# The channel factors of the first norm inside the split of x

## The chip, the core and the metric

The kernel runs on one core of a Trainium2 chip. The metric is the device time of one execution in microseconds, as the median of several. The core has five engines with a queue of instructions each: TensorE (PE; the loading of its stationary operand is shown apart as PEld), VectorE (DVE), ScalarE (ACT), GpSimd (POOL) and SyncE (SP), which here only issues DMA transfers. An engine takes its instructions in order, and waits where an operand isn't ready.

## The reference, cut to what matters

One transformer block on x of 1024 positions by 1024 channels, in float32. The change lies in the first norm and in the first projections:

```python
def rms_norm(x, g):
    y = x * lax.rsqrt(jnp.mean(x * x, axis=-1, keepdims=True) + EPS)
    return y * g

z = rms_norm(h, attn_norm) @ w_in                 # 1024 x 1024 @ 1024 x 2856
o_nsa = nsa_mixer(...)                            # compressed, selected and window attention, 8 heads
o_gla = gla_mixer(...)                            # gated linear attention, 4 heads
h = h + concat([o_nsa, o_gla]) @ w_out
u = causal_dwconv(rms_norm(h, ffn_norm) @ w_up, conv_w, conv_b)
gate, up = split(u)
h = h + (silu(gate) * up) @ w_down
```

## The kernel before

x is read transposed: a row tile `t` (8 of them, 128 positions each) lies in the core's memory as 128 partitions by 8 groups `k` of channels by 128 positions, so that the channel of a value is given by partition and group. `again` holds the factors of the norm in the same layout, 128 x 8. A product in nearly float32 is made of three products of the type float32r: each operand is split into a high part (`hi_of`, a copy on ScalarE that rounds to float32r, L57) and a low part (`lo_of`, value minus high part, L60, on VectorE or POOL), and `zmm` (L114 to L120) sums high times high (L118), high times low (L119) and low times high (L120) over the eight groups.

The norm's factor per row isn't applied to x: `x_stat` forms the sum of squares of a tile (a reduction on VectorE, L264; a product with ones, L265) and the root by a chain of small instructions on VectorE (`rsqrt`, L66 to L73), and `rx[:, t]` scales the results when they leave PSUM (`kcvc` L289, `gl` L290, `zqk` L201, `vv` L204). The factor per channel is applied to x before the split.

`x_first(t, eng)` (L248 to L259) makes the split tile `xt`: one transfer of 512 KB by SP into `xraw` (2 buffers), the squares `xsq` on ScalarE (1 buffer), the multiply of `xraw` by `again` in place on `eng` (VectorE for tile 0, POOL for the other seven), and then two halves of four groups each, split into high and low part by ScalarE and VectorE.

The stage around it first loads the weights `wA` (296 columns) in four pieces of two groups each, splits them (the low parts on VectorE and POOL in turn), and loads tile 0 ahead of the split of the first piece. Then it loads the eight pieces of `wC` (512 columns; low parts in turn on POOL and VectorE). In the loop over tiles it makes tile `t + 2` and its sum of squares, multiplies tile `t` by `wA` and by `wC`, evicts the results, and stores the split tile to `x_d` for later passes. The later passes (queries, linear attention, attention, and the feed-forward part) read `x_d` and don't call `x_first`.

The order in which an engine takes its instructions isn't that of the text: a scheduler lays out the queues from its own timing of the whole program, so instructions of later steps can stand ahead of earlier ones. Buffers are bound the same way; a load into a buffer waits for the last reader of what was there.

Of the kernel before, what the change touches and what calls it, by code (L numbers as in the profile page):

```python
# [7 lines left out]
F = mybir.dt.float32  # L8
R = mybir.dt.float32r
I32 = mybir.dt.int32  # L10
AF = mybir.ActivationFunctionType
OP = mybir.AluOpType
# [5 lines left out]
NT, NK = 8, 8  # L18
# [16 lines left out]
def body(tc, I, out, tap=lambda name, ap: None):  # L35
    nc = tc.nc
    V, A, P, T, SY = nc.vector, nc.scalar, nc.gpsimd, nc.tensor, nc.sync
# [18 lines left out]
    def hi_of(dst, src, scale=1.0):  # L56
        A.activation(dst, src, AF.Copy, scale=scale)  # L57

    def lo_of(dst, src, hi, eng=None):
        (eng or V).tensor_sub(dst, src, hi.bitcast(F))  # L60
# [19 lines left out]
    again = con.tile([128, NK], F, name="again")  # L80
# [8 lines left out]
    def split(dst_h, dst_l, src, eng=None):  # L89
        hi_of(dst_h, src)  # L90
        lo_of(dst_l, src, dst_h, eng)
# [5 lines left out]
    xtp = pool(sW, "xtp", XB)  # L97
# [60 lines left out]
    with ExitStack() as sp:  # L158
# [70 lines left out]
        def pair(t, z, qpass, kept=[]):  # L229
            kept.append((t, z))  # L230
            if len(kept) == 2:
                for (tt, zz), rr in zip(kept, norms([z for _, z in kept], 8 if qpass else 4)):
                    heads(tt, zz, rr, qpass)
                kept.clear()


        with ExitStack() as sx:
            wap = pool(sx, "wap", 1)
            xr_p = pool(sx, "xr_p", 2)
            xfp = pool(sx, "xfp", 2)  # L240
            ones = wap.tile([128, 1], F, name="ones")
            V.memset(ones, 1.0)
            wah = wap.tile([128, NK, NA], R, name="wah")
            wal = wap.tile([128, NK, NA], R, name="wal")
            WA = [(wah[:, k], wal[:, k]) for k in range(NK)]
            xts = {}

            def x_first(t, eng):  # L248
                raw = xr_p.tile([128, NK, 128], F, name="xraw")
                SY.dma_start(raw, I["xT"][t])  # L250
                sq = xr_p.tile([128, NK, 128], F, name="xsq", bufs=1)
                A.activation(sq, raw, AF.Square)
                eng.tensor_tensor(raw, raw, again[:, :, None].to_broadcast([128, NK, 128]), op=OP.mult)
                xt = []
                for i in range(2):
                    x = (xfp if i else xtp).tile([128, 2, 4, 128], R, name="xt")
                    split(x[:, 0], x[:, 1], raw[:, 4 * i:4 * i + 4], V)
                    xt.append(x)
                return xt, sq  # L259

            def x_stat(t, sq):
                st = pp.tile([128, 512], F, name="st", tag="h1", bufs=2)
                ssq = c2.tile([128, 128], F, name="ssq", tag="vv")
                V.tensor_reduce(ssq, sq.rearrange("p k t -> p t k"), axis=X, op=OP.add)  # L264
                T.matmul(st[:, 0:1], ssq, ones, start=True, stop=True)  # L265
                rsqrt(c2, rx[:, t:t + 1], st[:, 0:1], 1.0 / D, 1)

            for k2 in range(4):
                raw = wap.tile([128, 2, NA], F, name="araw", bufs=2)
                SY.dma_start(raw, I["wA"][k2])  # L270
                ks = slice(2 * k2, 2 * k2 + 2)
                if k2 == 0:
                    SY.dma_start(again, I["again"])
                    xts[0], sq = x_first(0, V)
                split(wah[:, ks], wal[:, ks], raw, P if k2 % 2 else V)
            x_stat(0, sq)
            WC = [w_load(I["wC"][1, k], 512, V if k % 2 else P) for k in range(NK)]
            for dst, name in ((ident, "ident"), (rope, "rope"), (hgain, "hgain")):
                SY.dma_start(dst, I[name])
            xts[1], sq = x_first(1, P)  # L280
            x_stat(1, sq)
            for t in range(NT):
                if t + 2 < NT:
                    xts[t + 2], sq = x_first(t + 2, P)
                    x_stat(t + 2, sq)
                xt = xts.pop(t)
                ps = zp.tile([128, 512], F, name="z")
                zmm(ps[:, :NA], xt, WA)
                V.tensor_scalar(kcvc[:, t], ps[:, :256], rx[:, t:t + 1], None, op0=OP.mult)  # L289
                V.tensor_scalar(gl[:, t], ps[:, 256:NA], rx[:, t:t + 1], None, op0=OP.mult)  # L290
                zq = zp.tile([128, 512], F, name="z")
                zmm(zq, xt, WC)
                for i in range(2):
                    A.dma_start(x_d[t, i].bitcast(F), xt[i].bitcast(F))
                pair(t, evac(t, zq, False), False)
            V.tensor_scalar(rxh, rx, 0.5, None, op0=OP.mult)
            V.tensor_scalar(rx8, rx, 0.125, None, op0=OP.mult)
# [89 lines left out]
        for t in range(NT):  # L387
            xt = x_load(x_d[t])
# [271 lines left out]
    k2 = pool(sK, "k2", 18, side="right")  # L660
# [30 lines left out]
    with ExitStack() as sp:  # L691
# [5 lines left out]
        for half in (1, 0):  # L697
            WO = WO_[half]
            for t in range(NT):
                if half and t in (4, 7):  # L700
                    WO_[0].append([w_load(I["wO"][t // 7, k], 512, V) for k in range(4)])
                if half and t == 7:

                    w0 = [facp["T3"].tile([128, 4, 512], R, name=f"w0{p}", tag=p) for p in "hl"]
                    for i in range(4):
                        raw = rawp.tile([128, 512], F, name="wraw")
# [3 lines left out]
                xt = xtp.tile([128, 2, 4, 128], R, name="xt")  # L710
# [432 lines left out]
```

## Time and profile before

| | |
|---|---|
| median of 3 executions | 1365.21 us (1365.13 to 1858.76) |
| the profiled execution | 1363.89 us |
| its span, first to last instruction | 1362.1 us |
| TensorE, VectorE busy | 96%, 79% of the span |
| ScalarE, POOL busy | 51%, 25% of the span |
| mean granted clock of TensorE | 0.991 of full speed |

The profile is of one execution. An engine's busy time is the union of its instructions; matmuls are pipelined, so a matmul's duration is longer than the distance to the next one, and the same holds by a little for VectorE and ScalarE. An idle stretch is put down to what ended it (the "releaser").

### The profile page before, as it was taken

The numbers are of one execution on the slowest core, as the hardware profiler recorded it, in microseconds if no ns is written. First come the engines' busy times: TensorE is split into PE (matmuls) and PEld (weight loads), VectorE is DVE, ScalarE is ACT, GpSimd is POOL, SyncE is SP. The second block draws the span as 40 slices with busy tenths as digits, with TensorE's granted clock in tenths as the row PEclk, the third lists the DMA queues.
The fourth block names the chain that finished last, engine by engine and source line by source line (L and its number), as shares of the span: only waits on it lengthen the run. The fifth ranks groups of instructions, "written<-read, shape, count | busy, mean of one in ns | idle before, by whom it ended". The sixth has DMA issues, their size and how long they took to land.

```text
span 1362.1 us, 19780 instructions
## 1 busy us (share of the span) xinstructions
PE 1312.4 (96%) x6618; PEld 1096.7 (81%) x6618; DVE 1077.5 (79%) x2530; ACT 701.0 (51%) x1383; POOL 334.0 (25%) x491
## 2 busy tenths in 40 slices
PE   6899989999999999999999999999999998999998
PEld 5787867888788887778788888888888886888887
DVE  7985865877878788982588998888788878699774
ACT  5342655767666567763464544444344444444431
POOL 4343653556644447432500000000000000000000
PEclk9999989999999999999999999999999998999999
DMA  8537673323422225012743122222222229664073
GB/s 306 199 109 263 180 243 101 106 91 117 138 66 83 73 81 157 31 46 67 246 145 112 50 105 93 77 78 94 85 86 76 79 78 349 243 203 155 34 238 115
DMA packets 80535, 177.07 MB, mean 130 GB/s; under 512 B 10785, under 2 KB 22962, under 8 KB 80434
## 3 DMA queue, kind: packets, MB, share of 16 engines
q1 hardware_dynamic: 54450, 111.84, 24.1%
q0 software_dynamic: 10368, 37.75, 9.0%
q10 hardware_dynamic: 15616, 26.22, 5.3%
q8 instruction: 52, 0.85, 0.3%
q14 instruction: 49, 0.40, 0.1%
HBM read 133.84 MB, written 41.94 MB: 129 GB/s over the span
## 4 chain that ended last, share of the span: by engine, by line
PE 82%; DVE 10%; DMA 3%; ACT 3%; issue 2%; POOL 1%; SPq 0%; ACTq 0%; POOLq 0%; DVEq 0%
PE pda L982 9%; PE pdb L982 7%; PE z L118 4%; PE z L119 4%; PE z L120 4%; PE O L466 4%; PE S L448 4%; PE pt L459 3%; PE uZ L679 3%; PE uX L680 3%; PE uX L679 3%; PE uX L681 3%; PE uZ L680 3%; PE uZ L681 3%; PE uW L680 3%; PE uW L681 3%
## 5 line engine op out<-in xcount | busy, mean ns | idle before, releaser
L118 PE MATMUL z<-whi,xt 128*128 128x512 f32 (+1 forms) x384 | 142.8, 372 | 6.5 <-DVE rs_i L67 2.8
L119 PE MATMUL z<-wlo,xt 128*128 128x512 f32 (+1 forms) x384 | 140.4, 366 | 0.1
L120 PE MATMUL z<-whi,xt 128*128 128x512 f32 (+1 forms) x384 | 140.1, 365 | 0.0
L60 DVE TENSOR_TENSOR PTl<-pt,PTh 128x512 fp32r<-128x512 f32 (+1 forms) x148 | 99.9, 684 | 32.8 <-ACT PTh L57 32.4
L453 ACT ACTIVATE P<-P,m 128x640 f32<-128x640 f32 (+7 forms) x128 | 94.1, 735 | 53.5 <-DVE m L450 52.1
L57 ACT ACTIVATE PTh<-pt 128x512 fp32r<-128x512 f32 (+1 forms) x148 | 85.3, 592 | 53.1 <-PE pt L459 50.4
L527 POOL TENSOR_SCALAR P<-P,sc 128x640 f32<-128x640 f32 (+7 forms) x128 | 89.4, 709 | 84.3 <-DVE sc L473 55.5
L448 PE MATMUL S<-kst,qst 128*128 128x320 f32 (+5 forms) x384 | 100.1, 352 | 3.9 <-DVE m L450 3.5
L57 ACT ACTIVATE wuh<-wuraw 128x512 fp32r<-128x512 f32 x65 | 40.5, 631 | 103.3 <-PE uZ L680 52.8
L118 PEld LDWEIGHTS z<-whi,xt 128*128 128x128 f32 x384 | 74.2, 193 | 17.3 <-issue 5.1
L459 PE MATMUL pt<-ident,P 128*128 128x128 f32 x528 | 86.5, 274 | 0.8 <-DVE PTl L60 0.6
L119 PEld LDWEIGHTS z<-wlo,xt 128*128 128x128 f32 x384 | 73.9, 193 | 9.9 <-DVE wlo L60 0.5
L120 PEld LDWEIGHTS z<-whi,xt 128*128 128x128 f32 x384 | 73.9, 192 | 9.9
L57 ACT ACTIVATE dh<-g 128x1024 fp32r<-128x1024 f32 x44 | 46.6, 1062 | 65.6 <-PE pdb L982 27.7
L57 ACT ACTIVATE wuh<-ws 128x512 fp32r<-128x512 f32 x76 | 47.6, 631 | 63.2 <-PE uW L680 29.2
L459 PEld LDWEIGHTS pt<-ident,P 128*128 128x128 f32 x528 | 66.1, 141 | 15.9 <-issue 1.4
L448 PEld LDWEIGHTS S<-kst,qst 128*128 128x128 f32 x384 | 62.5, 191 | 13.7 <-DVE m L450 8.1
L982 PE MATMUL pda<-dh 128*128 128x512 f32 x176 | 68.5, 390 | 0.0
L982 PE MATMUL pda<-dh,dl 128*128 128x512 f32 x176 | 68.4, 390 | 0.0
L982 PE MATMUL pda<-dl,dh 128*128 128x512 f32 x176 | 68.4, 390 | 0.0
L792 ACT ACTIVATE y<-u,cb,cw 128x1024 f32<-128x1024 f32 x44 | 54.3, 1240 | 20.9 <-DVE u L871 15.1
L450 DVE CUSTOM_DVE_ANT_0 P<-S,wmask 128x320 f32<-128x320 f32 (+4 forms) x96 | 46.0, 485 | 23.9 <-PE S L448 22.7
(474 smaller groups left out, 3956.3 us busy)
## 6 DMA issues: line engine op xcount, KB each, us to landing
xt<-x_d POOLq DMA_DIRECT2D x48, 512.0 KB, 3.7
wuraw<-in_wU_dram SPq DMA_DIRECT2D x42, 512.0 KB, 3.6
dv<-in_wD_dram SPq DMA_DIRECT2D x55, 256.0 KB, 3.2
act_d<-y SPq DMA_DIRECT2D x22, 512.0 KB, 2.6
dv<-act_d SPq DMA_DIRECT2D x44, 256.0 KB, 3.4
x_d<-xt ACTq DMA_DIRECT2D x16, 512.0 KB, 4.1
xt<-mix_d POOLq DMA_DIRECT2D x16, 512.0 KB, 4.1
g<-in_wD_dram SPq DMA_DIRECT2D x22, 256.0 KB, 5.6
```

The source lines that it names most:

```text
L57: A.activation(dst, src, AF.Copy, scale=scale)
L60: (eng or V).tensor_sub(dst, src, hi.bitcast(F))
L118: T.matmul(ps, x[:, 0], wh, start=(k == 0), stop=False)
L119: T.matmul(ps, x[:, 0], wl, start=False, stop=False)
L120: T.matmul(ps, x[:, 1], wh, start=False, stop=(k == NK - 1))
L448: T.matmul(ps[:, :e - c], qst[:, h], kcols(i, c, e), start=(i == 0), stop=(i == 1))
L453: A.activation(Pt, Pt, AF.Exp, bias=m, scale=-1.0, accum_out=sc)
L459: T.transpose(tp[:n, h], get(h), ident)
L527: P.tensor_scalar(Ps[hh][:, :n], Ps[hh][:, :n], sc[:, hh:hh + 1], 1.0, op0=OP.mult, op1=OP.mult)
L680: T.matmul(ps, wh[:, k], bl[:, k], start=False, stop=False, skip_group_check=True)
L681: T.matmul(ps, wl[:, k], bh[:, k], start=False, stop=(k == 3 and last), skip_group_check=True)
L982: T.matmul(ps[t], l[:, ts], r, start=(j == 0 and n == 0 and not add), stop=(j == NH - 1 and n == 2), skip_group_check=True)
```

## The change

`x_first` no longer takes an engine and no longer multiplies the tile. For each of the eight groups of a tile, ScalarE's copy for the high part takes the group's column of `again` as its scale per partition, and VectorE's subtraction becomes a fused instruction, `raw * again - high`. The squares come after the splits in the text. Tile 0 is loaded by two transfers of four groups each, and `again` is loaded ahead of the first piece of `wA`.

```diff
-            def x_first(t, eng):
+            def x_first(t):
                 raw = xr_p.tile([128, NK, 128], F, name="xraw")
-                SY.dma_start(raw, I["xT"][t])
+                xt = []
+                for i in range(2):
+                    ks = slice(4 * i, 4 * i + 4)
+                    if t == 0:
+                        SY.dma_start(raw[:, ks], I["xT"][t, :, ks])
+                    elif i == 0:
+                        SY.dma_start(raw, I["xT"][t])
+                    x = (xfp if i else xtp).tile([128, 2, 4, 128], R, name="xt")
+                    for k in range(4):
+                        g, r = again[:, 4 * i + k:4 * i + k + 1], raw[:, 4 * i + k]
+                        hi_of(x[:, 0, k], r, g)
+                        V.scalar_tensor_tensor(x[:, 1, k], r, g, x[:, 0, k].bitcast(F), op0=OP.mult, op1=OP.subtract)
+                    xt.append(x)
                 sq = xr_p.tile([128, NK, 128], F, name="xsq", bufs=1)
                 A.activation(sq, raw, AF.Square)
-                eng.tensor_tensor(raw, raw, again[:, :, None].to_broadcast([128, NK, 128]), op=OP.mult)
-                xt = []
-                for i in range(2):
-                    x = (xfp if i else xtp).tile([128, 2, 4, 128], R, name="xt")
-                    split(x[:, 0], x[:, 1], raw[:, 4 * i:4 * i + 4], V)
-                    xt.append(x)
                 return xt, sq
...
             for k2 in range(4):
+                if k2 == 0:
+                    SY.dma_start(again, I["again"])
                 raw = wap.tile([128, 2, NA], F, name="araw", bufs=2)
                 SY.dma_start(raw, I["wA"][k2])
                 ks = slice(2 * k2, 2 * k2 + 2)
                 if k2 == 0:
-                    SY.dma_start(again, I["again"])
-                    xts[0], sq = x_first(0, V)
+                    xts[0], sq = x_first(0)
                 split(wah[:, ks], wal[:, ks], raw, P if k2 % 2 else V)
...
-            xts[1], sq = x_first(1, P)
+            xts[1], sq = x_first(1)
             x_stat(1, sq)
             for t in range(NT):
                 if t + 2 < NT:
-                    xts[t + 2], sq = x_first(t + 2, P)
+                    xts[t + 2], sq = x_first(t + 2)
                     x_stat(t + 2, sq)
```

## Rows read from the trace of the kernel before

**Rows 1.** The page: the span, and TensorE's busy time, share and instructions.

```profile
span 1362.1 us, 19780 instructions
PE 1312.4 (96%) x6618; PEld 1096.7 (81%) x6618; DVE 1077.5 (79%) x2530; ACT 701.0 (51%) x1383; POOL 334.0 (25%) x491
```

**Rows 2.** Stretches: bounds and length, busy time by engine, granted clock, DMA share, GB/s.

```profile
0.00:10.00 10.00, 0.00 (x0) 0.00 (x0) 3.60 (x4) 5.41 (x8) 1.80 (x6) 1.00 0.77 251
...
22.00:80.00 58.00, 51.26 (x287) 44.29 (x287) 56.79 (x163) 25.31 (x46) 25.68 (x26) 1.00 0.58 206
80.00:105.00 25.00, 25.00 (x141) 21.83 (x140) 20.71 (x67) 11.22 (x23) 12.26 (x17) 1.00 0.40 136
```

**Rows 3.** Waits of TensorE to 130 us: waiter, releaser, total, times, longest.

```profile
PE z L118 <- ACT xt L57: 10.1, 1, 10.1
...
PE z L118 <- DVE rs_i L67: 2.8, 2, 2.0
PE z L118 <- DVE vv L204: 2.6, 1, 2.6
...
PE z L120 <- DVE xt L60: 1.1, 1, 1.1
```

**Rows 4.** Timeline of the first tile: start, duration, engine, line, out and in.

```profile
1.65 0.42 SPq L250 DMA_DIRECT2D xraw<-in_xT_dram  x1
...
6.14 1.06 ACT L252 ACTIVATE xsq<-xraw 128x1024 f32<-128x1024 f32 x1 [1.74 <-DMA xraw<-in_xT_dram]
7.23 1.23 DVE L253 TENSOR_TENSOR xraw<-xraw,again 128x1024 f32<-128x1024 f32 x1 [2.02 <-ACT xsq L252]
...
8.37 1.97 DVE L264 TENSOR_REDUCE ssq<-xsq 128x128 f32<-128x1024 f32 x1
...
9.45 1.14 ACT L57 ACTIVATE xt<-xraw 128x512 fp32r<-128x512 f32 x2
...
11.55 2.77 DVE L60 TENSOR_TENSOR xt<-xraw,xt 128x512 fp32r<-128x512 f32 x2
```

**Rows 5.** Timeline of VectorE: three neighbours, for the distance between starts.

```profile
54.91 0.18 DVE L193 TENSOR_TENSOR nm<-zqk,rope 128x32 f32<-128x32 f32 x1
55.02 0.68 DVE L60 TENSOR_TENSOR xt<-xraw,xt 128x512 fp32r<-128x512 f32 x1
55.62 0.69 DVE L60 TENSOR_TENSOR comb<-zqk,comb 128x512 fp32r<-128x512 f32 x1
```

**Rows 6.** Groups of VectorE by form, whole span: busy us, mean ns, idle before.

```profile
L613 DVE SCALAR_TENSOR_TENSOR og<-o,ro,gs 128x128 f32<-128x128 f32 x30 | 9.3, 344 | 0.2
```

**Rows 7.** POOL to 105 us: a group, then two lines of its timeline.

```profile
L253 POOL TENSOR_TENSOR xraw<-xraw,again 128x1024 f32<-128x1024 f32 x7 | 14.0, 1995 | 21.9 <-ACT xsq L252 21.9
...
30.70 1.90 POOL L253 TENSOR_TENSOR xraw<-xraw,again 128x1024 f32<-128x1024 f32 x1 [4.28 <-ACT xsq L252]
32.55 5.67 POOL L60 TENSOR_TENSOR wlo<-wraw,whi 128x512 fp32r<-128x512 f32 x4
```

**Rows 8.** Timeline of VectorE beside POOL's instructions with tensors in SBUF.

```profile
31.36 1.52 DVE L60 TENSOR_TENSOR Vst<-vv,Vst 128x256 fp32r<-128x256 f32 x1
...
35.27 1.82 DVE L60 TENSOR_TENSOR xt<-xraw,xt 128x512 fp32r<-128x512 f32 x1
...
37.38 1.39 DVE L60 TENSOR_TENSOR xt<-xraw,xt 128x512 fp32r<-128x512 f32 x1
...
67.96 1.74 DVE L77 SCALAR_TENSOR_TENSOR nrr<-rs_u,nrr 128x8 f32<-128x8 f32 x1
```

**Rows 9.** VectorE's timeline away from POOL, and a group of ScalarE.

```profile
42.37 0.41 DVE L60 TENSOR_TENSOR Vst<-vv,Vst 128x256 fp32r<-128x256 f32 x1
...
67.46 0.16 DVE L75 SCALAR_TENSOR_TENSOR rs_u<-nrr 128x8 f32<-128x8 f32 x1
...
L57 ACT ACTIVATE ch<-cr 128x128 fp32r<-128x128 f32 x1 | 0.3, 311 | 0.3 <-POOL cr L195 0.3
```

**Rows 10.** Timeline of POOL: an instruction of a later step.

```profile
12.74 1.05 POOL L305 TENSOR_SCALAR hgain<-hgain 128x512 f32<-128x512 f32 x1
```

## What I forecast, and why

> **What bounds the kernel now.** I read the page first, then the table of stretches, then the waits of TensorE (PE), then single instructions and groups of VectorE (DVE), ScalarE (ACT) and GpSimd (POOL) in the stretch that the change touches. The profiled execution took 1363.89 us, its span is 1362.1 us, and TensorE is busy 1312.4 us of that [rows 1]. So whatever the change does, it does to the 50 us in which TensorE has nothing to do, or it adds to them.
>
> The eight calls of `x_first` lie in the first 85 us. The table of stretches [rows 2] shows that in the first 10 us TensorE does nothing and VectorE is busy for 3.60 us only; that from 22 to 80 us VectorE has no slack (56.79 of 58.00 us) while TensorE has some (51.26) and ScalarE much (25.31); and that from 80 to 105 us TensorE is full (25.00 of 25.00). So up to 80 us VectorE sets the pace, and TensorE loses 6.7 us to it behind 22 us. TensorE's waits say the same [rows 3]: 10.1 us until the first high half of x exists, 1.1 us for a low half of x, and 2.8 and 2.6 us for VectorE's root chain and its eviction `vv`, which release the banks of `z`.
>
> After 105 us nothing of the change runs. A microsecond that VectorE saves before 80 us counts if TensorE's queue moves up by it; TensorE is full behind that, so the shift is carried on.
>
> **The first tile.** Before, the chain is this [rows 4]: x is issued at 1.65 and has landed at 6.14, when ScalarE squares it for 1.06 us; VectorE multiplies from 7.23 for 1.23 us; the two high halves start on ScalarE only at 9.45, the two low halves on VectorE only at 11.55, and these take 2.77 us, because POOL's splits of weights run beside the first of them. TensorE starts at 10.1 and then stands for the low half [rows 3].
>
> After, `again` is issued ahead of the first `wA` piece and the second half of x needs an issue of its own, 0.42 us each [rows 4]: two pieces of weights come that much later, one of them well before x, the other behind it. The first half of x is issued when the whole was; no row shows when half a tile lands. It is not before 4 us, if its time from issue shrinks with its size from 4.5 to 2.25 us, and not after 6.14. I take 5.3. ScalarE's eight small high halves then run from 5.3 to about 7.5 and VectorE's eight low halves right behind them, in time in which VectorE was idle [rows 2]. The square ends at about 8.3, and VectorE's reduction starts where it started before (8.37 [rows 4]). TensorE's first work is at about 5.7 us. VectorE's queue behind 10 us loses the 2.77 us of the two low halves: **-2.8 us**. The multiply lay before 10 us, beside idle time, and brings nothing more.
>
> **Tiles 1 to 7 on VectorE.** Per tile, two subtractions of 128x512 become eight fused multiply-subtracts of 128x128. A subtraction of 128x512 lasts 0.68 us and its follower starts 0.60 us after it; one of 128x32 lasts 0.18 us and its follower starts 0.11 us after it [rows 5]. So an instruction holds the engine for its duration less 0.08. The new form isn't in this stretch. The nearest row is the fused instruction of the same shape at L613, 344 ns in the mean, one of whose operands comes from PSUM [rows 6]: 0.26 us each. Below that, the line through 128x32 and 128x512 gives 0.28, so 0.20 us each; above it, the full 0.344 without overlap. 56 of them at 0.26 are 14.6 us, 14 subtractions at 0.60 were 8.4 us: **+6.2 us** (from +2.8 to +10.9).
>
> The Trainium skill, "VectorE: DVE Perf Modes", section "The TRN2 errata", speaks against this part: an instruction that reads SBUF pays a fixed extra latency, so tiles of 512 elements or more are asked for, and VectorE is given 58 cycles plus the columns at 0.96 GHz. By that (an estimate) 56 at 194 ns against 14 at 594 ns cost +2.5 us, at the lower end of the term above, and the whole sum would be -6.3 us.
>
> **The multiply on POOL.** Seven multiplies of 128x1024, 14.0 us, leave POOL [rows 7]. POOL has room, but its multiply holds VectorE: while it runs, a VectorE instruction with two tensor operands in SBUF ends only with it. POOL's multiply from 30.70 lasts 1.90 us, and the subtraction for Vst that VectorE starts in it at 31.36 takes 1.52 us [rows 7, 8], elsewhere 0.41 [rows 9]. This happens under five of the seven multiplies; the last is a root step of 128x8 that takes 1.74 us [rows 8] instead of 0.16 [rows 9]. The five losses are 1.1, 1.5, 1.2, 1.6 and 1.6 us: **-7.0 us** of VectorE's time. The other two multiplies met only instructions with one tensor operand, which they don't hold.
>
> **What the small pieces lose to POOL.** POOL keeps its splits of weights: four in a row from 32.55 take 5.67 us [rows 7], and two low halves of x beside them took 1.82 and 1.39 us instead of 0.68 [rows 8]. If each POOL instruction holds one VectorE instruction to its end, four small pieces can lose what two large ones lost. Bounds: nothing (without the multiplies POOL is ahead, and its splits may fall elsewhere), and 4 x 1.4 - 1.85 = +3.8 us for this group. I take **+1.0 us**, nearer to nothing, because it is one such group in 58 us.
>
> **ScalarE and the queues.** 64 high halves of 128x128 replace 16 of 128x512. A copy of 128x128 at the same line lasts 0.31 us [rows 9]; two of 128x512 take 1.14 us together [rows 4]. With the same overlap of 0.1 us eight small ones take 1.7 to 2.5 us: +0.6 to +1.4 us per tile, 5 to 11 us in all. I count nothing, for ScalarE has 33 of 58 us free between 22 and 80 us [rows 2]; without that cover these 5 to 11 us would be the price. The square is moved behind the eight, and with it the reduction and the root chain of its tile, by about 2 us; they are formed two tiles ahead of their use. In exchange the multiply between square and split goes, so the split starts about 3 us sooner after x has landed. SP's next load of x waits for the low halves and the square of an earlier tile; both end no later. No transfer is added after tile 0.
>
> **Sum:** -2.8 + 6.2 - 7.0 + 1.0 = -2.6 us, and 1363.89 - 2.6 = 1361.3 us. The median of the runs shown, 1365.21, lies 1.3 us above the profiled execution, so I forecast 1362 us.
>
> **The rivals.**
> A, *TensorE takes the early start in full*. The 10.1 us shrink to about 5.7, the 1.1 us go, and half of the 6.7 us behind 22 us go with VectorE's held instructions: -4.4 - 1.1 - 3.4 = -9, 1356 us. For it: VectorE and TensorE have idle time before 10 us [rows 2]. Against it: what TensorE multiplies next are pieces of weights that land later and are split by the same engines, so the time won at the start may be spent waiting for them. Chance 0.25.
>
> B, *slower: the small pieces run into POOL's splits*. POOL and VectorE exclude each other by instruction [rows 7, 8], and x now offers 64 instructions that can be caught instead of 16. The fixed part alone is +6.2; if 4 to 8 us instead of 1.0 are lost to POOL's splits, the sum is +0.4 to +4.4, and with the upper bound of the fused instruction up to +9: 1366 to 1374 us. It decides where the loss to POOL passes 3.6 us; then VectorE is busy longer and the waits for `vv` and the roots grow. The Trainium skill, "SBUF — State Buffer", section "SBUF: two separate sides", has this as an exclusive lock that whoever starts first holds for its whole instruction; the pairs above agree (0.16 becoming 1.74). Chance 0.2.
>
> C, *nothing*. VectorE's savings end in waits of its own and TensorE's gaps stay, hung on ScalarE or on weights: 1364 to 1366 us. Chance 0.15.
>
> **Numbers.** The forecast has 0.4; its own range is 1358 to 1364 us. The engines' order of instructions is laid out anew with the change (POOL runs L305 at 12.74, far ahead of its place in the text [rows 10]), and this can add or take some us in places that I can't see. From A with 3 us beyond it to the middle of B, which the bounds of the fused instruction (-3.4 and +4.7 about its term) fill: 1353 to 1372 us. Two per cent, about what a measurement of this kernel can tell from no change, are 27 us, and no case comes near them: faster 0.02, same 0.96, slower 0.02.
>
> **What would show it.** Right: a first matmul before 7 us; fused instructions of about 0.34 us spaced by 0.26; no VectorE instruction of 1.5 us or more where the multiplies were; VectorE's busy time from 22 to 80 us about as before. Wrong: fused instructions of 0.4 us in the mean, many of them over 1 us beside POOL's splits; TensorE idle for well over 6.7 us between 22 and 80 us, or with ScalarE as what it waits for; or a change of more than 10 us that arises behind 105 us, where nothing was edited.

## The result, and the profile after

The changed kernel takes 1376.03 us (median of 6 executions, 1374.25 to 1381.7) against 1365.22 us for the kernel before: a ratio of 1.0087, with a 95% interval from 1.0074 to 1.0099. That is 11 us slower by the medians and some 12 by the ratio, which leaves out one execution of the kernel before of 1858.76 us; it lies outside the forecast range and on the other side of it. Two per cent is not reached. The profiled execution took 1376.87 us, 13 us more than the profiled execution of the kernel before.

The page of the changed kernel, to be set beside [rows 1]: TensorE is busy 9.6 us longer, though it has the same 6618 products.

```profile
span 1375.1 us, 19869 instructions
PE 1322.0 (96%) x6618; PEld 1101.2 (80%) x6618; DVE 1083.6 (79%) x2577; ACT 712.1 (52%) x1431; POOL 321.9 (23%) x484
```

The same three stretches as in [rows 2] (bounds and length, busy time of PE, PEld, DVE, ACT, POOL, granted clock, DMA share, GB/s), with two of the first 28 us between them:

```profile
0.00:10.00 10.00, 2.57 (x8) 1.90 (x8) 4.13 (x11) 6.60 (x14) 0.76 (x5) 1.00 0.79 252
...
16.00:22.00 6.00, 2.74 (x12) 2.17 (x11) 5.55 (x15) 6.00 (x16) 0.77 (x1) 0.86 1.07 386
22.00:28.00 6.00, 4.88 (x13) 3.24 (x13) 5.90 (x11) 3.46 (x8) 3.25 (x3) 0.50 0.70 245
...
22.00:80.00 58.00, 52.99 (x265) 45.03 (x265) 53.00 (x179) 29.18 (x71) 13.62 (x21) 0.87 0.52 180
80.00:105.00 25.00, 25.00 (x145) 22.00 (x145) 22.12 (x77) 10.83 (x23) 7.30 (x14) 1.00 0.28 96
```

Between 22 and 80 us VectorE is *less* busy than before (53.00 against 56.79 us) and TensorE more (52.99 against 51.26 us), yet TensorE has started 265 products there and not 287. Its granted clock is 0.87 in the mean, and 0.50, the lower of its two levels (1.2 GHz), from 22 to 28 us. ScalarE, whose work I had counted at nothing, is busy in every moment from 16 to 22 us.

TensorE's waits to 130 us, to be set beside [rows 3] (releaser, total, times, longest):

```profile
PE z L118 <- ACT xt L57: 5.8, 1, 5.8
...
PE st L271 <- DVE ssq L270: 3.8, 2, 3.3
PE z L118 <- DVE vv L204: 3.2, 1, 3.2
PE z L118 <- ACT wah L57: 1.6, 1, 1.6
PE z L119 <- DVE wlo L60: 1.1, 1, 1.1
```

The first wait fell from 10.1 to 5.8 us, as forecast. A new one of 3.3 us stands below it: TensorE waits for tile 1's sum of squares.

**Where the 13 us come from.** Two points cut the run. The first product S of the attention with the compressed keys (`kcT`) ends everything that the change could touch directly; the last product O with `Vst` ends attention and linear attention. The rows of single lines give the first and the last start (durations in ns as least, median and most; the line of S is L448 before and L455 after, that of O L466 and L473). Before:

```profile
L448 PE MATMUL S<-kcT,qst x128: 191/277/382, 204.2 to 586.2; 128*128 128x64 f32 x128
L466 PE MATMUL O<-PTl,Vst x132: 388/476/589, 225.7 to 641.6; 128*128 128x512 f32 x132
```

After:

```profile
L455 PE MATMUL S<-kcT,qst x128: 192/277/382, 211.9 to 600.8; 128*128 128x64 f32 x128
L473 PE MATMUL O<-PTl,Vst x132: 387/400/775, 231.8 to 653.7; 128*128 128x512 f32 x132
```

So 7.7 us are lost ahead of the first S (204.2 to 211.9), and 4.4 us more between the first S and the last O (437.4 us before, 441.8 after), in a stage in which not a line was edited. Of the 7.7 us, 7.1 are lost by the first product `h` of the step behind the projections (113.2 us before, 120.3 after). The remaining 0.9 us lie behind the last O. They are two losses with two causes, and the experiments take them one at a time.

### The profile page after: what moved, and what is told of

It reads as the page before. It is cut to its first block, busy times and chain, and to the rows that moved or that the text cites. A ratio compares the mean times of both kernels' runs of the same rounds, so it can differ in the third digit from the quotient of the medians.

```text
span 1375.1 us, 19869 instructions
## 1 busy us (share of the span) xinstructions
PE 1322.0 (96%) x6618; PEld 1101.2 (80%) x6618; DVE 1083.6 (79%) x2577; ACT 712.1 (52%) x1431; POOL 321.9 (23%) x484
## 4 chain that ended last, share of the span: by engine, by line
PE 75%; DVE 11%; DMA 5%; issue 3%; ACT 2%; POOL 2%; SPq 0%; ACTq 0%; POOLq 0%; DVEq 0%
PE pda L989 9%; PE pdb L989 7%; PE z L118 4%; PE z L120 4%; PE z L119 4%; PE O L473 4%; PE S L455 4%; PE pt L466 3%; PE uX L687 3%; PE uX L686 3%; PE uX L688 3%; PE uW L688 3%; PE uZ L688 3%; PE uW L686 3%; PE uZ L686 3%
## 5 line engine op out<-in xcount | busy, mean ns | idle before, releaser
L455 PE MATMUL S<-kst,qst 128*128 128x320 f32 (+5 forms) x384 | 100.0, 353 | 3.2 <-DVE m L457 2.4
L466 PE MATMUL pt<-ident,P 128*128 128x128 f32 x528 | 86.0, 275 | 1.0 <-DVE PTl L60 0.8
L120 PEld LDWEIGHTS z<-whi,xt 128*128 128x128 f32 x384 | 73.8, 192 | 10.1 <-issue 0.2
L466 PEld LDWEIGHTS pt<-ident,P 128*128 128x128 f32 x528 | 66.2, 141 | 15.6 <-PE S L455 1.5
L455 PEld LDWEIGHTS S<-kst,qst 128*128 128x128 f32 x384 | 63.9, 193 | 15.0 <-DVE m L457 8.5
L473 PE MATMUL O<-PTl,Vst 128*128 128x512 f32 x132 | 58.6, 444 | 6.0 <-DVE PTl L60 5.8
```

The lines of the kernel that those rows point to most:

```text
L120: T.matmul(ps, x[:, 1], wh, start=False, stop=(k == NK - 1))
L455: T.matmul(ps[:, :e - c], qst[:, h], kcols(i, c, e), start=(i == 0), stop=(i == 1))
L466: T.transpose(tp[:n, h], get(h), ident)
L473: T.matmul(O, Vt, y[:n], start=(nmm[0] == 0), stop=(nmm[0] == total - 1))
```

## The experiments

All ratios are to the kernel before, with 95% intervals. "First S" and "S to O" are read from one profiled execution each; executions of one kernel spread by several us, so a difference of 1 or 2 us in them says nothing (the one of the filled gap took 8.7 us more than the median of its kernel).

| kernel | ratio | first S, us | S to O, us |
|---|---|---|---|
| before | 1 | 204.2 | 437.4 |
| changed | 1.0087 [1.0074, 1.0099] | 211.9 | 441.8 |
| first tile alone | 1.0063 [1.0044, 1.0082] | 211.0 | 444.8 |
| later tiles alone | 1.0006 [0.9989, 1.0023] | 201.0 | 441.8 |
| squares ahead of the splits | 1.0038 [1.0023, 1.0054] | 207.3 | 441.8 |
| splits of `wA` and `wC` on VectorE | 1.0057 [1.0041, 1.0073] | 207.7 | 445.4 |
| tile 2's transfer held | 1.0053 [1.0032, 1.0075] | 208.3 | 441.8 |
| the same, `again` second | 0.9998 [0.9986, 1.0010] | 206.8 | 436.1 |
| before, `again` first | 1.0022 [1.0010, 1.0035] | 203.9 | 441.2 |
| before, an idle transfer | 1.0066 [1.0046, 1.0086] | 212.1 | 441.9 |
| TensorE's gap filled | 1.0059 [1.0039, 1.0078] | 209.2 | 450.8 |
| tile 1 behind the fourth `wA` | 1.0034 [1.0018, 1.0050] | 202.1 | 445.2 |
| later tiles, `again` by POOL | 0.9972 [0.9954, 0.9989] | 202.9 | 435.2 |
| tile 0 whole, tile 1 behind `wA` | 0.9994 [0.9982, 1.0007] | 208.8 | 435.9 |

### Which part: the first tile or the later ones

The new `x_first` (here `x_new`) and the old one (`x_old`) stand side by side, and each kernel takes one for tile 0 and the other for tiles 1 to 7. First tile alone:

```diff
-                    xts[0], sq = x_first(0)
+                    xts[0], sq = x_new(0)
...
-            xts[1], sq = x_first(1)
+            xts[1], sq = x_old(1, P)
```

> Only tile 0 is made in the new way (halves, factors inside the split, factors loaded first); tiles 1 to 7 are made as before, with the multiply on POOL and lows of 128x512. Theory L: no small pieces beside POOL's splits, so the loss goes, and the early start of TensorE stays: 1358 to 1365 us. Theory Q: TensorE starts at 5.8 us, has done what is there by 18 us and then stands with its clock falling, whatever the later tiles do: 1370 to 1376 us, TensorE idle for over 2 us between 17 and 23 us and a granted clock under 0.9 in 22 to 50 us.

Later tiles alone (`again` loaded where it was before):

```diff
-                    xts[0], sq = x_first(0)
+                    SY.dma_start(again, I["again"])
+                    xts[0], sq = x_old(0, V)
...
-            xts[1], sq = x_first(1)
+            xts[1], sq = x_new(1)
```

> Tile 0 is made as before (one transfer, multiply on VectorE, lows of 128x512, factors loaded behind the first weights); tiles 1 to 7 in the new way. Theory L: the loss is all here, 1372 to 1378 us. Theory Q: TensorE starts at 10 us as before and finds work until the next tile is there, so it doesn't stand at 18 us and the clock stays: 1363 to 1368 us.

The first tile alone has the first S at 211.0 us, 6.8 us later than before: nearly the whole of the first loss. The later tiles alone have it at 201.0, 3.2 us *earlier* than before. So the part that I had priced with care, the small fused instructions against POOL's multiply, does no worse than the sum said (+0.2), and the loss sits in the part that I had booked as a gain. Both medians, 1375.78 and 1366.81 us, lie in theory Q's ranges and outside theory L's.

### Which step of the first tile

Squares ahead of the splits, as they were:

```diff
+                sq = xr_p.tile([128, NK, 128], F, name="xsq", bufs=1)
+                A.activation(sq, raw, AF.Square)
                 for i in range(2):
...
-                sq = xr_p.tile([128, NK, 128], F, name="xsq", bufs=1)
-                A.activation(sq, raw, AF.Square)
                 return xt, sq
```

> The change with one thing undone: the square of a tile stands ahead of its eight small splits in the text again. Theory Q (queues: TensorE's product with ones for the sum of squares of tile 1 stands in its queue and waits 3.3 us at 18 us for a square that comes behind eight splits; then the granted clock is low until 34 us): that wait shrinks to under 1.5 us, and the time falls by 4 to 8 us, to 1368 to 1372. Theory L (the small fused instructions are held by POOL's splits, 7 us of VectorE's time): nothing of that is touched, 1374 to 1378 us, with as many fused instructions over 0.6 us as now.

All splits of this stage's own weights on VectorE, so that POOL keeps only the four splits of the next weights there (30.80 to 35.95 us):

```diff
-                split(wah[:, ks], wal[:, ks], raw, P if k2 % 2 else V)
+                split(wah[:, ks], wal[:, ks], raw, V)
...
-            WC = [w_load(I["wC"][1, k], 512, V if k % 2 else P) for k in range(NK)]
+            WC = [w_load(I["wC"][1, k], 512, V) for k in range(NK)]
```

> The change, with the low parts of wA and wC all on VectorE, so that POOL has nothing beside VectorE while x is split before 45 us. VectorE gets six more subtractions, about 4 us. Theory L: no fused instruction over 0.6 us, 7 us less of loss against 4 us of work: 1371 to 1375 us. Theory Q: VectorE has more to do before the sums of squares, TensorE waits for them as long or longer: 1376 to 1381 us.

The first S comes at 207.3 and at 207.7 us: each gives back somewhat over half of the 7.7 us, and neither all of it. In both, TensorE still stands over 3 us in one piece at a product for a sum of squares (3.6 and 3.4 us), where theory Q had asked for under 1.5 with the squares first. Nor is the second run free of POOL: its fused instructions take 398 ns in the mean, against 451 in the changed kernel, and six of them more than 0.6 us, the longest beside the four splits that are left. So the order of the squares and POOL's hold on VectorE both carry part of the loss; the next two tests ask what stands ahead of them. It shows in SP's queue, of which the changed kernel has these rows (start, duration, queue, line, transfer; all transfers of x by L256 are whole tiles):

```profile
9.55 1.18 SPq L256 DMA_DIRECT2D xraw<-in_xT_dram  x2
...
12.62 0.33 SPq L278 DMA_DIRECT2D araw<-in_wA_dram  x1
13.05 0.44 SPq L101 DMA_DIRECT2D wraw<-in_wC_dram  x1
```

and the kernel before these, with ScalarE's among them:

```profile
8.27 0.33 SPq L250 DMA_DIRECT2D xraw<-in_xT_dram  x1
...
10.30 0.33 SPq L270 DMA_DIRECT2D araw<-in_wA_dram  x1
...
14.73 1.06 ACT L252 ACTIVATE xsq<-xraw 128x1024 f32<-128x1024 f32 x1 [2.52 <-DVE rs_a L66]
15.40 1.36 SPq L250 DMA_DIRECT2D xraw<-in_xT_dram  x1
15.69 0.68 ACT L57 ACTIVATE wah<-araw 128x592 fp32r<-128x592 f32 x1
...
17.80 1.16 ACT L57 ACTIVATE xt<-xraw 128x512 fp32r<-128x512 f32 x2 [0.91 <-POOL xraw L253]
```

Before, tile 1 is issued at 8.27 us, the fourth piece of `wA` at 10.30, and tile 2 only at 15.40. In the changed kernel tile 0 is split early, its buffer is free early, and tile 2 goes out right behind tile 1 (from 9.55), ahead of that piece (12.62). Tile 1 stood ahead of the piece before as well; new is tile 2. ScalarE shows the second half of the story. Before, it squares tile 1 at 14.73, and while POOL multiplies the tile it rounds the fourth piece of `wA` (15.69); tile 1's high halves follow at 17.80. In the changed kernel nothing comes between:

```profile
16.00 2.45 ACT L57 ACTIVATE xt<-xraw,again 128x128 fp32r<-128x128 f32 x8 [3.97 <-DMA xraw<-in_xT_dram]
18.35 1.04 ACT L264 ACTIVATE xsq<-xraw 128x1024 f32<-128x1024 f32 x1
...
19.30 1.26 ACT L57 ACTIVATE xt<-xraw,again 128x128 fp32r<-128x128 f32 x4
20.46 0.69 ACT L57 ACTIVATE wah<-araw 128x592 fp32r<-128x592 f32 x1
```

Eight small copies of tile 1, its square, four copies of tile 2, and only then, at 20.46 us, the weights without which tile 0 can't be finished. How long the piece was on its way shows in the trace, as the time from its issue to its landing, before and then after:

```profile
DMA to landing us min/median/max: 4.1/4.1/4.1
```

```profile
DMA to landing us min/median/max: 5.7/5.7/5.7
```

So does what SP waited for ahead of it in the changed kernel, and when that was issued:

```profile
SPq L278 <- DMA x_d<-xt: 0.7, 1, 0.7
```

```profile
7.23 0.35 ACTq L301 DMA_DIRECT2D x_d<-xt  x1
```

So the piece is rounded 4.8 us later than before (20.46 against 15.69), and this has three parts. It is issued 2.3 us later, in the end because SP waits for the landing of tile 0's own store to `x_d`, which an early tile 0 sends out early (7.23 us, before 13.34). It is 1.6 us longer on its way, with the two tiles issued ahead of it. And from landing (18.35) to rounding 2.1 us pass in ScalarE's queue, where before it was 1.3. TensorE, which had started 4.3 us sooner, stands:

```profile
17.75 0.40 PE L120 MATMUL z<-whi,xt 128*128 128x512 f32 x1
21.41 0.58 PE L271 MATMUL st<-ones,ssq 128*128 128x1 f32 x2 [3.26 <-DVE ssq L270]
```

### Tile 2's transfer

The changed kernel, with tile 2's transfer behind the last piece of `wC` on SP's queue:

```diff
                     elif i == 0:
-                        SY.dma_start(raw, I["xT"][t])
+                        with tc.issue_after(loads[-1].ins) if t == 2 else ExitStack():
+                            SY.dma_start(raw, I["xT"][t])
```

> The change, with tile 2's transfer queued on SP behind the eighth piece of wC, where it stood before the change. In the changed kernel tile 0's raw buffer is free at 8.7 us instead of 14.3, so SP issues tile 2's load at 10.4 us, ahead of the last piece of wA and of wC's second half, and its splits stand ahead of theirs. Theory P (that place of tile 2 starves TensorE from 18 us on): TensorE finds work behind 18 us, the first attention product S starts at 198 to 204 us instead of 211.9, and the whole takes 1364 to 1369 us, because the attention stage keeps its new order. Theory Q (TensorE's early start by itself: its queue is drained by 18 us and the sum of squares of tile 1 comes late behind the splits): S from 209 us on, 1373 to 1377 us.

The other way round, the kernel before with 512 KB that nobody reads, at the place where the changed kernel has tile 2:

```diff
-                SY.dma_start(raw, I["xT"][t])
+                xl = SY.dma_start(raw, I["xT"][t])
+                if t == 1:
+                    with tc.issue_after(xl.ins):
+                        SY.dma_start(kcvc[:, 4:8].rearrange("p t (a s) -> p (t a) s", a=2), I["xT"][2])
```

> The kernel before, with a transfer of 512 KB that nobody reads (tile 2 of x into a buffer that is written later) queued on SP behind tile 1's, where the changed kernel has tile 2's. No engine but the DMA has more to do. The attention stage gets the other order too. If the displaced bytes alone starve TensorE: the last piece of wA and the second half of wC land 1.5 us or more later and the first S starts 3 to 8 us later than 204.2. If it is the work on tile 2 that stands in the engines' queues ahead of the weights: the first S within 2 us of 204.2, and the whole slower only by the other order's 3 to 5 us.

Held back, the transfer gives 3.6 us (first S at 208.3), about half, and not the 198 to 204 us of theory P. Added to the kernel before, it costs 7.9 us (212.1), as much as the change, though by a way of its own: its TensorE loses little until 38 us, and then stands 3.8 us for a sum of squares. So the order of transfers here is worth that much, but tile 2 alone is not the cause.

### Tile 1's transfer

The changed kernel, with tile 1's transfer behind that of the fourth piece of `wA`:

```diff
-                SY.dma_start(raw, I["wA"][k2])
+                wl = SY.dma_start(raw, I["wA"][k2])
...
                     elif i == 0:
-                        SY.dma_start(raw, I["xT"][t])
+                        with tc.issue_after(wl.ins) if t == 1 else ExitStack():
+                            SY.dma_start(raw, I["xT"][t])
```

> The changed kernel, with the transfer of row tile 1 held on SP's queue behind that of the fourth piece of wA. In the kernel before, ScalarE rounds this piece at 15.69 us, while POOL multiplies tile 1; in the changed kernel tile 1 (16.00) and tile 2 (19.30) come first on ScalarE, and the piece is rounded at 20.46. Theory (tile 0's short path lets tiles 1 and 2 run ahead of weights that TensorE needs sooner): the piece is rounded by about 15 us, TensorE has its work of tile 0 with all of wA and doesn't stand for 3 us before 22 us, the clock stays at 1.00 to 30 us, and the first product of the attention comes at 204 to 208 us instead of 211.9; 1368 to 1372 us. Rival (whatever comes first, 10 to 28 us is full with transfers, so the start that TensorE won is lost as a stall in another place, with the low clock behind it): a stall of 3 us or more on another operand before 40 us, clock 0.50 for some us behind it, first product of the attention at 210 to 213 us and 1374 to 1377 us.

```profile
12.87 0.34 SPq L279 DMA_DIRECT2D araw<-in_wA_dram  x1
...
14.41 0.33 SPq L257 DMA_DIRECT2D xraw<-in_xT_dram  x1
...
16.40 0.70 ACT L57 ACTIVATE wah<-araw 128x592 fp32r<-128x592 f32 x1 [4.20 <-DMA araw<-in_wA_dram]
...
18.91 2.45 ACT L57 ACTIVATE xt<-xraw,again 128x128 fp32r<-128x128 f32 x8 [1.22 <-DMA xraw<-in_xT_dram]
```

The piece is issued no sooner (12.87), but it lands before tile 1, 3.5 us after its issue, and ScalarE rounds it at 16.40 instead of 20.46. Tile 2 stays behind tile 1 and so moves too, from 10.33 to 16.45 us: the run shows what the two tiles cost ahead of that piece, and not what each does. The first S comes at 202.1 us: 9.8 us are back, and the first stage is now 2.1 us shorter than before. That this is near the -2.6 of my sum proves little, for the kernel before was not run with the piece ahead of the tile. By the ratios (1.0087 to 1.0034) 7 us are back. A stall of 3.0 us for tile 1's sum of squares came all the same, at 27 us and no longer at 18, so the theory was right in the result and wrong in that detail; with all of tile 0 done by then, it cost less than it gave.

### TensorE's clock

In the changed kernel the granted clock is 0.59 from 20 to 22 us and 0.50 from 22 to 34 us, behind the stall of 3.26 us, so the low clock was a suspect of its own. Ahead of 17 us the clock's column reads 1.00, but the products say otherwise: in the changed kernel those of 512 columns start 0.42 us apart there, and 0.24 us apart behind 17 us,

```profile
14.22 0.63 PE L119 MATMUL z<-wlo,xt 128*128 128x512 f32 x1
14.64 0.63 PE L120 MATMUL z<-whi,xt 128*128 128x512 f32 x1
...
17.29 0.40 PE L118 MATMUL z<-whi,xt 128*128 128x512 f32 x1
17.53 0.39 PE L119 MATMUL z<-wlo,xt 128*128 128x512 f32 x1
```

and in the kernel before 0.42 us to 17.70 and 0.23 from 18.66 us on. TensorE thus began at the lower level in both, and its start 4.3 us sooner brought the full clock only about 1 us sooner. To test what the fall at 20 us costs, 14 products of 128x512 whose results nobody reads fill the stall here:

```diff
                 ssq = c2.tile([128, 128], F, name="ssq", tag="vv")
                 V.tensor_reduce(ssq, sq.rearrange("p k t -> p t k"), axis=X, op=OP.add)
+                if t == 1:
+                    y = xts[1][0][:, 0]
+                    for _ in range(14):
+                        T.matmul(st, y[:, 0], y, start=True, stop=True)
                 T.matmul(st[:, 0:1], ssq, ones, start=True, stop=True)
```

> The changed kernel with 14 products of 128x512 that nobody reads, put on TensorE just ahead of the product for tile 1's sum of squares, where the changed kernel's TensorE stands for 3.26 us (17.75 to 21.41). They take about 14 x 0.21 = 3.0 us at the full clock, so TensorE does the same useful work as before and only stops standing. Theory (the stall itself costs little, because the loads behind set the pace until 20 us anyway; the loss is the granted clock of 0.50 from about 20 to 34 us that follows the stall): the clock stays near 1.00 from 20 to 34 us, TensorE goes through the 12 us' work in about half the time as far as weights are there, and the first product of the attention comes at 205 to 208 us instead of 211.9; the run is 4 to 6 us shorter than the changed kernel's, about 1371 us. Rival (the stall and what is late behind it, the loads and ScalarE's queue, are the loss; the low clock only fills time that TensorE would have waited): the first product of the attention stays at 211 to 213 us, whatever the clock does, and the run stays at 1375 to 1377 us.

```profile
20.00:22.00 2.00, 1.32 (x8) 0.85 (x6) 2.00 (x2) 2.00 (x5) 0.78 (x1) 1.00 1.08 404
22.00:24.00 2.00, 1.29 (x7) 0.71 (x5) 2.00 (x2) 2.00 (x4) 2.00 (x3) 1.00 1.00 375
24.00:26.00 2.00, 1.24 (x3) 0.49 (x3) 1.93 (x6) 0.17 (x1) 1.26 (x1) 0.63 0.14 57
26.00:28.00 2.00, 1.21 (x3) 0.83 (x3) 1.96 (x5) 1.28 (x4) 0.00 (x0) 0.50 0.84 275
```

The stall is gone and the clock stays at 1.00 to 24 us, 4 us longer. Then it falls all the same, TensorE being busy about two thirds of the time, and is 0.50 to 34 us. What counts is the work done. Adding up the columns of TensorE's products started by a given time, from their records in the trace (without the 14 idle ones):

```
by, us          20      28      36      40
before       11474   26630   43486   46664
changed      11474   16836   26334   27654
gap filled   11474   16836   25742   32390
x1 behind wA 14274   26628   31238   39344
```

At 20 us the changed kernel, for all its early start, has done exactly as much as the one before (at 18 us it was ahead, 11474 against 7138; then it stood). At 28 us the filled one has done exactly as much as the unfilled, though its clock was about twice as fast from 20 to 24 us: between 20 and 28 us weights and operands set the pace, and the clock doesn't. The first S comes 2.7 us sooner (209.2; by the ratios 3.8 us), which arises behind 36 us. A count at 40 us doesn't foretell the first S: the last row, behind the first one from 30 us on, is ahead of it by 80 us (119694 against 118414, and 107150 in the changed kernel). So each theory has a part, and the larger part is with the rival: what is late are the loads and ScalarE's queue. How much of the rest is the clock's stays open, for no version of the changed kernel here kept it at 1.00 through 34 us with the changed order of loads. The kernel before with the idle transfer did (1.00 from 17 to 41 us) and lost as much, in a later stall with the low clock behind it (0.50 from 41 to 48 us).

### The attention stage

This stage falls into two groups. Whether S to O takes 435 to 437 us or 441 and more goes with the order in which the scheduler laid it out: comparing TensorE's queues line by line from the first S on, the kernel before, the one with `again` second, the one with `again` by POOL and the one with tile 0 whole have the very same order, and all others share a second one. The first test is the kernel before with `again` loaded first, and nothing else changed:

```diff
             for k2 in range(4):
+                if k2 == 0:
+                    SY.dma_start(again, I["again"])
                 raw = wap.tile([128, 2, NA], F, name="araw", bufs=2)
                 SY.dma_start(raw, I["wA"][k2])
...
-                    SY.dma_start(again, I["again"])
                     xts[0], sq = x_first(0, V)
```

> The kernel before, with the factors (4 KB) loaded ahead of the first piece of wA and nothing else changed. The scheduler lays out the attention stage in the other order for that. Theory R: the first S starts within 2 us of 204.2, the last linear-attention step leaves about 87 us of attention instead of 73, and the whole is 3 to 5 us slower, 1368 to 1371 us. Otherwise: 1365 to 1367 us.

```profile
L449 PE MATMUL S<-kcT,qst x128: 191/277/400, 203.9 to 592.2; 128*128 128x64 f32 x128
L467 PE MATMUL O<-PTl,Vst x132: 388/400/628, 224.1 to 645.1; 128*128 128x512 f32 x132
```

Moving a transfer of 128 x 8 numbers, 0.42 us of SP's time, leaves the first S where it was (203.9), and lengthens the stage by 3.8 us: 1.0022. The opposite test is the kernel with tile 2's transfer held, and `again` back in second place:

```diff
-                if k2 == 0:
-                    SY.dma_start(again, I["again"])
                 raw = wap.tile([128, 2, NA], F, name="araw", bufs=2)
                 SY.dma_start(raw, I["wA"][k2])
...
+                    SY.dma_start(again, I["again"])
                     xts[0], sq = x_first(0)
```

> As the run with tile 2's transfer held, and the factors are loaded second again, as before the change. With that the scheduler lays out the attention stage in the order of the kernel before (its last linear-attention step ends later, and fewer products are left behind it); with the factors first it lays it out otherwise. Theory R (the other order of the attention stage costs 3 to 5 us, whatever the first stage does): the first S as in that run, the last S earlier by 3 to 5 us, 1358 to 1363 us. If the order costs nothing: the same as that run within 1 us.

It has the order of before, 436.1 us and not 441.8, and the ratio goes from 1.0053 to 0.9998. By the ratios that is 7.5 us, more than the stage's 5.7, and the median of 1366.58 us is still above the 1358 to 1363 that theory R asked for. A third test takes the later tiles alone and loads `again` by POOL's queue:

```diff
-                    SY.dma_start(again, I["again"])
+                    P.dma_start(again, I["again"])
                     xts[0], sq = x_old(0, V)
```

> Tiles 1 to 7 with the new form, tile 0 with the old (as in the experiment on the later tiles alone), and the 128 x 8 channel factors loaded by POOL's queue in place of SP's. By that the scheduler lays out attention and linear attention in the order of the kernel before, not in that of the changed kernel. Theory (the loss in that stage comes from its order and not from the edit, and the later tiles' new form gains 3 us): first product of the attention at about 201 us, 436 to 437 us from there to the last product with V instead of 442.2, 1360 to 1362 us, ratio 0.996 to the kernel before. Rival (the stage is longer with the new form for another reason, such as the state that it leaves on the queues): 441 to 443 us for that stage, 1366 to 1368 us.

435.2 us for the stage against 441.8, and 0.9972 [0.9954, 0.9989] against 1.0006: the one version here that beats the kernel before, by about 4 us. What the second order costs is read from the end of the stage, and not tested by itself. From 550 to 655 us, before and then after:

```profile
550.00:655.00 105.00, 101.00 (x523) 79.32 (x522) 64.04 (x218) 58.37 (x127) 38.54 (x47) 1.00 0.20 64
```

```profile
550.00:655.00 105.00, 97.52 (x507) 75.21 (x507) 72.17 (x240) 61.07 (x132) 33.76 (x44) 0.98 0.13 41
```

and the largest wait of TensorE between 440 and 655 us in the changed kernel, which in the kernel before is 1.4 us (5 times):

```profile
PE O L473 <- DVE PTl L60: 5.4, 8, 1.9
```

The linear attention gives TensorE work that needs little of VectorE. In the second order it is finished sooner (last product `cu` at 567.1 us, 86.6 us ahead of the last O; before, 568.6 and 73.0), and for that much longer the attention has nothing beside it: VectorE is busier there (72.17 against 64.04 us), and TensorE waits for its low parts.

### Both repairs together

Tile 1's transfer behind the fourth piece of `wA`, and tile 0 by one transfer; the second edit gives the attention stage the order of before:

```diff
-                    if t == 0:
-                        SY.dma_start(raw[:, ks], I["xT"][t, :, ks])
-                    elif i == 0:
-                        SY.dma_start(raw, I["xT"][t])
+                    if i == 0:
+                        with tc.issue_after(wl.ins) if t == 1 else ExitStack():
+                            SY.dma_start(raw, I["xT"][t])
```

> The changed kernel with tile 1's transfer behind the fourth piece of wA, and with tile 0 loaded by one transfer instead of two halves. The second edit leads the scheduler to the order of attention and linear attention that the kernel before has. Theory (the two causes are the order of transfers in the first 20 us and the order of the attention stage, and nothing else in the change costs time): TensorE starts 1 to 2 us later than with halves, at 7 to 8 us, which is lost in later waits anyway; the first product of the attention comes at 202 to 204 us, 436 to 438 us from there to the last product with V, 1361 to 1363 us, ratio 0.995 to 0.998. Rival (the gain of 9.8 us in the first stage hung on the halves): the first product of the attention at 206 us or more, 1365 us or more, ratio at least 1.000.

0.9994 [0.9982, 1.0007]: the loss is gone (12 us by the ratios), and the gain that the theory asked for, 0.995 to 0.998, is not there. The stage took 435.9 us, as it said. The first S came at 208.8, as the rival had it; but this execution took 1370.44 us, 4.7 above the median of its 12, and 5.6 us of it are one wait of the step between the two stages (the first `h` for VectorE's `tb`), which is 3.1 us before. So whether tile 0's halves are worth 2 us is left open.

## Why the prediction was wrong

**What held.** The first matmul came at 5.83 us (forecast 5.7). The fused instruction lasts 0.33 to 0.35 us undisturbed (0.344), and two in a row take 0.61, so the second starts 0.27 behind the first (0.26). POOL's multiply no longer holds VectorE: the subtraction for `Vst` takes 415 ns in the mean to 112 us, and 803 before. For tiles 1 to 7 on their own the sum +6.2 - 7.0 + 1.0 = +0.2 was, if anything, too high: the later tiles alone gain 3.2 us to the first S.

**The term that was mis-sized.** The loss of small pieces to POOL's splits, +1.0. In the kernel with the later tiles alone the 56 instructions take 362 ns in the mean, 18 over their median of 344: 1.0 us in all, as forecast. In the changed kernel 64 take 451, 105 over their median of 346:

```profile
21.23 1.44 POOL L60 TENSOR_TENSOR wal<-araw,wah 128x592 fp32r<-128x592 f32 x1 [5.86 <-ACT wah L57]
22.64 2.60 POOL L60 TENSOR_TENSOR wlo<-wraw,whi 128x512 fp32r<-128x512 f32 x2
```

```profile
21.28 4.38 DVE L261 SCALAR_TENSOR_TENSOR xt<-xraw,again,xt 128x128 fp32r<-128x128 f32 x4
```

Four pieces that take 1.12 us where these splits are not on POOL take 4.38 beside three of POOL's. Over all, 64 times 105 ns are 6.7 us, past the 3.6 from which rival B was to decide. The Trainium skill, "SBUF — State Buffer", section "SBUF: two separate sides", has the lock by which each waits for the other's whole instruction; these rows agree (the first piece, begun at 21.28, ends at 22.83, and POOL's first split at 22.67). So rival B's condition came true. But its reason is not the first one: with the splits of `wA` and `wC` off POOL somewhat over half of the first loss is back; the collision itself comes from the late weights, since POOL splits them at 21 us only because ScalarE rounded them at 20.46; and with tile 1 behind the fourth piece, POOL keeping all its splits, the mean is 383 ns (2.4 us in all) and the first S comes 9.8 us sooner.

**The step that failed** is in "ScalarE and the queues", twice. I wrote that SP's next load of x waits for the low halves and the square of an earlier tile, and that "both end no later. No transfer is added after tile 0." The square alone ends later (8.77 us against 7.20). The last of the two, which decides, ends *sooner* (8.77 against 14.32), and that was what to follow: what was waiting for it, the 512 KB of tile 2, went out ahead of weights (10.33 against 15.40). Tile 0's store went out sooner with it, and SP had to wait for that store's landing before the fourth piece of `wA`. I had named the load as waiting, and not asked what it would overtake when released. And I counted ScalarE's 5 to 11 us at nothing for the cover of 33 free us between 22 and 80 us, where the price fell due between 16 and 22 us: there the changed kernel's ScalarE is busy 6.00 of 6.00 us, and the fourth piece, landed at 18.35, waits 2.1 us for it. Both together, with the collisions, stalls and low clock that follow from them, cost 7.7 us to the first S; how they share it is not shown. The multiply on POOL, which I booked only as a burden on VectorE, had been the pause in which ScalarE rounded that piece.

**The first tile's -2.8** was worked out for VectorE's queue. TensorE's columns show that nothing of it was left by 20 us: 11474 in both kernels. Rival A had the reason written against it (the pieces of weights land later, and the time won may be spent waiting), and that is what happened; I let it limit the gain, and did not follow it on to a loss.

**The attention stage.** That the order is laid out anew and can add some us "in places that I can't see" was said, and stood in the range with no size. In S to O it measured 3.8, 5.7 and 6.6 us in the three tests; by the ratios 3.0 (1.0022), 7.5 (1.0053 to 0.9998) and 4.6 us (1.0006 to 0.9972). Without it the changed kernel would have been at about 1369 to 1373 us, an estimate from these: at the edge of the range, and still on the wrong side.

## What to carry to other kernels

When an edit frees a buffer sooner, ask which transfer was held by it, and what that transfer will pass on the queue, and the same of a store that can go sooner; a prefetch that was late may have been late to the kernel's good. Read an engine's slack in the few microseconds where the moved work falls due, not over the stage. And where a scheduler lays out the queues, compare the order of stages that were not edited before looking there for a cause: moving one load of 0.42 us was worth 3 us, 200 us later.

## What was not expected of the hardware

A copy on ScalarE of 128x128 with a factor per partition follows the one before at 0.30 us (eight in 2.45 us), and two of 128x512 take 1.16: in eight pieces the same tile costs ScalarE twice the time.

The granted clock fell to 0.50 behind TensorE's stalls at a sum of squares, of 3.3 us in the changed kernel (22 to 34 us) and of 3.0 with tile 1 held (30 to 36 us). It fell too in the kernel with the gap filled, where the longest wait was 1.5 us (26 to 34 us), and in the kernel before with `again` first, behind a wait of 1.9 us (39.6 to 42.9 us). In the kernel before it stayed at 1.00 from 18 to 113 us, with waits of 2.0 and 2.6 us. So the length of a single wait doesn't tell these cases apart.

The Trainium skill, "VectorE: DVE Perf Modes", section "The TRN2 errata", gives 58 cycles and the columns at 0.96 GHz, an estimate of 194 ns for the fused 128x128, and adds that this row comes out too low for the duration of a single instruction; the trace has 0.27 us from one to the next and 0.34 for one alone, so here the small pieces cost more than by that row.
